# Seven products of quarter sums in place of eight in three groups of a down projection, computed in two column halves

## The chip, the cores and the metric

One Trainium2 chip, one core. The metric is the device time of one execution in microseconds (us). Engines are named as in the profile: PE (TensorE matmul), PEld (its weight loads), DVE (VectorE), ACT (ScalarE), POOL (GpSimd), SP (SyncE, which here only issues DMAs).

## What is computed

The reference is one layer of a hybrid decoder trunk on 256 tokens of 2048 features, in float32: a mixer part (gated linear attention and pooling, one combined input projection, one output projection), then a gated MLP, then a last RMS norm. The change lies in the MLP and the norm behind it:

```python
h = rmsnorm(x, norm_ffn_w[l])
gate, up = jnp.split(jnp.einsum('bsd,df->bsf', h, w_up[l]), 2, axis=-1)
gate = causal_dwconv(gate, conv_ffn_w[l]) + conv_ffn_b[l]
x = x + jnp.einsum('bsf,fd->bsd', jax.nn.gelu(gate, approximate=False) * up, w_down[l])
return rmsnorm(x, norm_final_w)
```

`w_up` is 2048 x 11264 and `w_down` is 5632 x 2048. The down projection multiplies the hidden values (256 x 5632) by `w_down`.

## The kernel before

Every float32 matrix product is made of three products in a rounded 32-bit format: each operand is split into a high and a low part, and high x high, low x high and high x low are summed in PSUM.

**Weights.** `srcs` lists all weight tiles of the kernel in the order in which they are used. One tile is 256 rows by 512 columns, held as 128 x 2 x 512. `load` (L125) brings it with one 512 KB DMA on SP's queue into `raw` (four buffers). `begin` makes two tiles of it: ACT copies it into `whi` (L158), and DVE subtracts to get `wlo` (L166). There are three buffers of each. `weights()` hands out the next pair and starts those two ahead (`AHEAD = 2`). So a tile's cast waits until PE has used the tile three before it.

**Order.** A scheduler fixes the order of instructions on each engine when the kernel is built, by its own estimate of times. On the chip each engine follows that order, and waits at semaphores.

**Up projection.** For each of 11 chunks of 512 features (four feature blocks of 128) `gemm_b` (L221, L222) forms the gate and then the up part, feature-major, 16 input blocks each, from the normalised features `fhl` (high and low part side by side, 16 blocks in one tile). DVE and ACT then do the convolution, the Gelu and the product (L1116 to L1128), and split the result `gs` into `hhi[c]` and `hlo[c]` (L1135, L1136), each 128 features x 4 blocks x 256 tokens.

**Down projection.** Here the hidden values are the stationary operand (128 features x 128 tokens) and the weights move, 512 columns at a time. The output is 4 columns of 512 by 2 token blocks of 128, and each of the 8 has a PSUM bank (`acc`: four from `psg`, four from `psm`). The loop runs over 22 pairs of feature blocks `kp` outside and over the four columns `c` inside, with one weight tile for each. `down_part` (L1154) uses a tile for both token blocks:

```python
for kk in range(2):
    k = 2 * kp + kk
    for n, (w, part) in enumerate(((hi, lh), (hi, ll), (lo, lh))):
        mm(ps[:, cs], part(k, t), w[:, kk, cs], ...)
```

That is 2 blocks x 3 passes x 2 token blocks = 12 products for a tile. The four tiles of the last pair are converted early (`KEEP`, `khi` and `klo`) and kept in buffers whose hidden values are no longer needed.

**End.** The last two pairs are done for one token block after the other, so that one block of tokens is normalised and stored while the other is multiplied. As a column's bank is complete, DVE adds it, scaled, to the residual `xt` (L1207), ACT squares and sums it (L1214), and DVE multiplies by the norm's weight `nfin` (L1216). The last block of 512 columns is done as two halves of 256. Then the sum of squares becomes the factor (L1203, L1204, L1211 on DVE, a power on POOL, L1217), the columns are scaled (L1182 to L1186) and stored (L1188).

Of the kernel before, what the change touches and what calls it, by code (L numbers as in the profile page):

```python
# [14 lines left out]
P = 128  # L15
# [20 lines left out]
def kernel(  # L36
# [32 lines left out]
    def nm(s):  # L69
        cnt[0] += 1  # L70
        return f"{s}_{cnt[0]}"
# [27 lines left out]
    LAST = KF // 2 - 1  # L99
    KEEP = (9, 12, 15, 18)  # L100
    kept = {}
    for kp in range(LAST):
        srcs += [down[c][kp] for c in range(4)]
        if kp in KEEP:
            kept[len(srcs)] = KEEP.index(kp)
            srcs.append(down[KEEP.index(kp)][LAST])
# [15 lines left out]
    def load_part(n, k):  # L122
        if n == len(loads):
            loads.append(wpool.tile(list(srcs[n].shape), F32, tag="raw", name=nm("raw"), bufs=4))
        last_load[0] = nc.sync.dma_start(loads[n][:, k], srcs[n][:, k]).ins  # L125

# [23 lines left out]
    def begin(n):  # L150
        while len(made) < min(len(srcs), n):
            load(len(made) + 1)
            raw = loads[len(made)]
            shape = list(raw.shape)
            keep = kept.get(len(made))
            hi = wpool.tile(shape, F32R, tag="whi", name=nm("whi")) if keep is None else \
                mtile(keep, shape, F32R, nm("khi"))
            nc.scalar.copy(hi, raw)  # L158
            if shape[1] == 8:
                lo = None  # L160
                nc.vector.tensor_tensor(hi[:, :, 32:64], raw[:, :, 0:32], hi[:, :, 0:32].bitcast(F32),
                                        op=ALU.subtract)
            else:
                lo = wpool.tile(shape, F32R, tag="wlo", name=nm("wlo")) if keep is None else \
                    mtile(4 + keep, shape, F32R, nm("klo"))
                last_split[0] = nc.vector.tensor_tensor(lo, raw, hi.bitcast(F32), op=ALU.subtract).ins  # L166
                splits.append(last_split[0])
            made.append((hi, lo))
# [123 lines left out]
    xhl = big.tile([P, KD, 2, S], F32R, tag="xhl", name="xhl")  # L292
    xhi, xlo = xhl[:, :, 0, :], xhl[:, :, 1, :]
# [11 lines left out]
    def parts_x(pts):  # L305
        for k, pt in pts:
            hi = nc.scalar.activation(xhi[:, k, :], pt, AF.Copy, scale=nmw[:, k : k + 1])
            lo = nc.vector.scalar_tensor_tensor(xlo[:, k, :], pt, nmw[:, k : k + 1], xhi[:, k, :].bitcast(F32),
                                                op0=ALU.mult, op1=ALU.subtract)
        return hi.ins, lo.ins  # L310
# [8 lines left out]
    def xh(k, t):  # L319
        return xhi[:, k, t * P : (t + 1) * P]  # L320

    def xl(k, t):
        return xlo[:, k, t * P : (t + 1) * P]
# [159 lines left out]
    for c in range(2):  # L483
        hi, lo = weights()
        for kk in range(8):
            k = 8 * c + kk
            mm(pba, hi[:, kk, :], xhl[:, k], start=(k == 0), stop=(k == KD - 1))
# [591 lines left out]
    fhl = big.tile([P, KD, 2, S], F32R, tag="xhl", name="fhl")  # L1079
    fhi, flo = fhl[:, :, 0, :], fhl[:, :, 1, :]  # L1080
    ssq4 = cpool.tile([P, 2, 4], F32, tag="ssq4", name="ssq4b")
    for c in range(4):
# [9 lines left out]
        for k2 in range(2):  # L1092
# [5 lines left out]
            for kk in range(2):  # L1098
                k = 4 * c + 2 * k2 + kk
                nw = vec[:, V_FFN + k : V_FFN + k + 1]  # L1100
                nc.scalar.activation(fhi[:, k, :], pt[:, kk, :], AF.Copy, scale=nw)
                nc.vector.scalar_tensor_tensor(flo[:, k, :], pt[:, kk, :], nw, fhi[:, k, :].bitcast(F32),
# [8 lines left out]
    hlo = []  # L1111
    rb2b = rb2.unsqueeze(1).to_broadcast([P, 4, S])
    for c in range(DFF // 512):
        ps = gemm_b(lambda k: fhl[:, k], KD)
# [12 lines left out]
        ps = gemm_b(lambda k: fhl[:, k], KD)  # L1127
# [10 lines left out]
        hlo.append(hl)  # L1138

    nfin = big.tile([P, D], F32, tag="xhl", name="nfin")  # L1140
    nc.scalar.dma_start(nfin, norm_final_w.partition_broadcast(P))
    acc = [[pg() for t in range(2)] for c in range(2)]
    for c in range(2):
        ps = pm()
        acc.append([ps[:, t, :] for t in range(2)])
    lh, ll = at(hhi), at(hlo)

    def down_part(kp, c, t, hi, lo, cs=slice(0, 512), ps=None, first=0):
        last_block = c == 3 and t == 1 and ps is None
        ps = acc[c][t] if ps is None else ps  # L1150
        for kk in range(2):
            k = 2 * kp + kk
            for n, (w, part) in enumerate(((hi, lh), (hi, ll), (lo, lh))):
                mm(ps[:, cs], part(k, t), w[:, kk, cs], start=(k == first and n == 0),  # L1154
                   stop=(k == KF - 1 and n == 2), skip_group_check=last_block)

    wk = []
    for kp in range(LAST - 1):
        for c in range(4):
            w = weights()  # L1160
            for t in range(2):
                down_part(kp, c, t, *w)
        if kp in KEEP:
            wk.append(weights())
    ws = []
    for c in range(4):
        ws.append(weights())
        if c == 0:
            for t in range(2):
                down_part(LAST - 1, c, t, *ws[c])  # L1170


    ssq5 = cpool.tile([P, 2, 5], F32, name="ssq5")
    part = cpool.tile([P, 2], F32, name="part")
    rs = cpool.tile([P, 2], F32, name="rsf")
    for t in range(2):
        ts = slice(t, t + 1)

        def scaled(c, by, queue):
            xs = xt[:, t, c * 512 : (c + 1) * 512]  # L1180
# [9 lines left out]


        blocks = [(c, slice(0, 512), None) for c in range(4 - t)]
        if t:
            blocks += [(3, slice(0, 256), None), (3, slice(256, 512), acc[0][0])]
        for n, (c, cs, ps) in enumerate(blocks):
            more = {} if ps is None else dict(ps=ps, first=2 * (LAST - 1))
            if c:
                down_part(LAST - 1, c, t, *ws[c], cs, **more)
            down_part(LAST, c, t, *wk[c], cs, **more)
            last = n == len(blocks) - 1  # L1200
            if last:

                nc.vector.tensor_reduce(part[:, ts], ssq5[:, t, 0:n], axis=mybir.AxisListType.X, op=ALU.add)  # L1203
                nc.vector.tensor_scalar(part[:, ts], part[:, ts], 1.0 / D, EPS, op0=ALU.mult, op1=ALU.add)  # L1204
            xs = xt[:, t, c * 512 : (c + 1) * 512]
            sums = cs if ps is not None else slice(0, 512)
            nc.vector.scalar_tensor_tensor(xs[:, sums], (acc[c][t] if ps is None else ps)[:, sums], rs2[:, ts],  # L1207
                                           xs[:, sums], op0=ALU.mult, op1=ALU.add)
            jk = cpool.tile([P, 512], F32, tag="sqj", name=nm("sqj"))
            if last:  # L1210
                nc.vector.tensor_tensor_reduce(jk[:, cs], xs[:, cs], xs[:, cs], scale=1.0 / D, scalar=part[:, ts],  # L1211
                                               op0=ALU.mult, op1=ALU.add, accum_out=rs[:, ts])
            else:
                nc.scalar.activation(jk[:, cs], xs[:, cs], AF.Square, accum_out=ssq5[:, t, n : n + 1])  # L1214
            if c < 3:
                nc.vector.tensor_tensor(xs, xs, nfin[:, c * 512 : (c + 1) * 512], op=ALU.mult)  # L1216
# [36 lines left out]
```

## Time and profile before

| what | value |
|---|---|
| device time, median of 3 runs | 1559.78 us (1559.38 to 1561.17) |
| span of the profiled execution | 1557.7 us |
| its own device time | not recorded apart; the median of the runs is 2.1 us above its span |
| PE busy | 1548.7 us (99%) |
| DVE busy | 1087.0 us (70%) |
| ACT busy | 748.2 us (48%) |
| HBM read and written | 299.66 MB and 5.28 MB |

The span runs from the first to the last instruction. In the rows of the profile, `out<-in` names tiles as the program does, `128x512` is partitions by elements, `x864` is the number of instructions, and what follows `<-` at the end is what ended the idle time before them. A line is that of the statement, and can be a helper's: L1154 is every product of the down projection.

### The profile page before, as it was taken

The page shows a single profiled execution, that of the slowest core. Times are in us where ns is not written, and L with a number is a line of the kernel's source. Part 1 is how long each engine was busy: PE and PEld are TensorE (multiplying, and loading weights), DVE is VectorE, ACT ScalarE, POOL GpSimd, SP SyncE. Part 2 cuts the span into 40 slices and gives each one's busy share as a digit, 9 for nine tenths or more (in the row PEclk, how much of TensorE's full clock was granted, in tenths as well). Part 3 has the DMA queues.
Part 4 walks back from the last instruction along what each step waited for, and adds up shares of the span by engine and source line. Part 5 has one row for each costly group of instructions (what it writes and reads, how often), then busy time and mean ns, then how long its engine had stood idle before and what let it go on. Part 6 is the DMA issues. An engine that isn't in the chain of part 4 may idle for free.

```text
span 1557.7 us, 21155 instructions
## 1 busy us (share of the span) xinstructions
PE 1548.7 (99%) x7966; PEld 1300.2 (83%) x7966; DVE 1087.0 (70%) x1676; ACT 748.2 (48%) x964; POOL 44.6 (3%) x54
## 2 busy tenths in 40 slices
PE   9999999999999999999999999999999999999998
PEld 8878888888878888888888888888888888888886
DVE  6788858996689859896656666776676667444445
ACT  6445446454545446354544544444444444434443
POOL 1010002000100000000000000000000000000000
PEclk9999999999999999999999999999999999999999
DMA  8776757766677656665655655555556656556662
GB/s 278 212 223 206 198 164 224 220 198 178 180 229 210 199 163 215 218 194 176 213 186 178 193 188 189 188 189 189 189 189 189 190 190 212 194 195 208 200 224 91
DMA packets 169108, 306.33 MB, mean 197 GB/s; under 512 B 19330, under 2 KB 23202, under 8 KB 168878
## 3 DMA queue, kind: packets, MB, share of 16 engines
q1 hardware_dynamic: 165984, 299.95, 61.4%
q10 hardware_dynamic: 3022, 5.03, 1.0%
q8 instruction: 62, 1.02, 0.3%
q14 instruction: 40, 0.33, 0.1%
HBM read 299.66 MB, written 5.28 MB: 196 GB/s over the span
## 4 chain that ended last, share of the span: by engine, by line
PE 98%; issue 1%; DMA 1%; DVE 0%; ACT 0%; POOL 0%; POOLq 0%; DVEq 0%
PE psm L199 15%; PE psm L197 15%; PE psm L198 15%; PE psm L221 11%; PE psg L221 10%; PE psg L1154 7%; PE psm L1154 7%; PE psg L222 5%; PE psm L222 5%; PE psm L333 1%; PE psg L242 1%; PE psg L723 1%; PE psg L725 0%; DMA vrow<-ev 0%; PE psg L861 0%
## 5 line engine op out<-in xcount | busy, mean ns | idle before, releaser
L166 DVE TENSOR_TENSOR wlo<-raw,whi 128x1024 fp32r<-128x1024 f32 x522 | 636.7, 1223 | 376.7 <-ACT whi L158 374.4
L158 ACT CAST whi<-raw 128x1024 fp32r<-128x1024 f32 x524 | 551.0, 1053 | 688.0 <-PE psm L198 282.7
L199 PE MATMUL psm<-wlo,xhl 128*128 128x512 f32 x864 | 339.6, 393 | 0.3 <-DVE wlo L166 0.3
L197 PE MATMUL psm<-whi,xhl 128*128 128x512 f32 x864 | 338.6, 392 | 0.0
L198 PE MATMUL psm<-whi,xhl 128*128 128x512 f32 x864 | 337.9, 391 | 0.0
L221 PE MATMUL psm<-fhl,whi 128*128 128x512 f32 x704 | 246.2, 396 | 0.0
L221 PE MATMUL psg<-fhl,whi 128*128 128x512 f32 x704 | 238.0, 394 | 0.0
L222 PE MATMUL psm<-fhl,wlo 128*128 128x256 f32 x704 | 194.3, 279 | 0.0
L199 PEld LDWEIGHTS psm<-wlo,xhl 128*128 128x128 f32 x864 | 162.3, 188 | 34.6 <-DVE wlo L166 1.5
L198 PEld LDWEIGHTS psm<-whi,xhl 128*128 128x128 f32 x864 | 162.3, 188 | 33.5
L197 PEld LDWEIGHTS psm<-whi,xhl 128*128 128x128 f32 x864 | 162.3, 188 | 33.3 <-issue 0.2
L222 PE MATMUL psg<-fhl,wlo 128*128 128x256 f32 x704 | 178.8, 279 | 0.0
L221 PEld LDWEIGHTS psm<-fhl,whi 128*128 128x128 f32 x704 | 131.4, 188 | 30.5
L221 PEld LDWEIGHTS psg<-fhl,whi 128*128 128x128 f32 x704 | 129.2, 188 | 24.1
L222 PEld LDWEIGHTS psg<-fhl,wlo 128*128 128x128 f32 x704 | 132.5, 188 | 6.9
L222 PEld LDWEIGHTS psm<-fhl,wlo 128*128 128x128 f32 x704 | 132.6, 188 | 1.1
L1154 PE MATMUL psg<-whi,hhi 128*128 128x512 f32 (+1 forms) x170 | 66.0, 388 | 0.0
L1154 PE MATMUL psg<-whi,hlo 128*128 128x512 f32 (+1 forms) x170 | 65.9, 388 | 0.0
L1154 PE MATMUL psm<-whi,hlo 128*128 128x512 f32 x168 | 65.1, 388 | 0.0
L1154 PE MATMUL psm<-wlo,hhi 128*128 128x512 f32 x168 | 65.1, 388 | 0.0
L1154 PE MATMUL psm<-whi,hhi 128*128 128x512 f32 x168 | 65.1, 388 | 0.0
L1154 PE MATMUL psg<-wlo,hhi 128*128 128x512 f32 (+1 forms) x170 | 59.6, 388 | 0.0
(278 smaller groups left out, 1505.9 us busy)
## 6 DMA issues: line engine op xcount, KB each, us to landing
raw<-in_w_in_dram SPq DMA_DIRECT2D x224, 512.0 KB, 4.2
raw<-in_w_up_dram SPq DMA_DIRECT2D x176, 512.0 KB, 4.5
raw<-in_w_down_dram SPq DMA_DIRECT2D x88, 512.0 KB, 4.3
raw<-in_w_out_dram SPq DMA_DIRECT2D x32, 512.0 KB, 3.6
mv<-vrow SPq DMA_DIRECT2D x12, 512.0 KB, 4.9
taps<-in_conv_qkv_w_dram SPq DMA_DIRECT2D x16, 256.0 KB, 6.4
raw<-in_pool_w_dram SPq DMA_DIRECT2D x8, 512.0 KB, 4.0
crow<-crd SPq DMA_DIRECT2D x4, 512.0 KB, 4.1
```

Of the source, the lines that this page charges most:

```text
L158: nc.scalar.copy(hi, raw)
L166: last_split[0] = nc.vector.tensor_tensor(lo, raw, hi.bitcast(F32), op=ALU.subtract).ins
L197: mm(ps[:, t, :], lh(k, t), hi[:, kk, :], start=(k == 0), stop=False)
L198: mm(ps[:, t, :], ll(k, t), hi[:, kk, :], start=False, stop=False)
L199: mm(ps[:, t, :], lh(k, t), lo[:, kk, :], start=False, stop=(k == nk - 1))
L221: mm(ps[f], hi[:, kk, fs], rhl(k), start=(k == 0), stop=False, skip_group_check=True)
L222: mm(ps[f][:, 1, :], lo[:, kk, fs], rhl(k)[:, 0, :], start=False, stop=(k == nk - 1), skip_group_check=True)
L242: nc.tensor.transpose(pt[:, ff, t * P : (t + 1) * P], src[:, t, f * P : (f + 1) * P], ident)
L333: mm(ps_k0[:, t, :], part(k, t), w[:, kk, :], start=(k == 0 and w is hi and part is xh), stop=(k == KD - 1 and w is lo))
L723: mm(pg0, kq[:, h, 0, 0:P], kq[:, h, :, :], start=True, stop=True)
L1154: mm(ps[:, cs], part(k, t), w[:, kk, cs], start=(k == first and n == 0), stop=(k == KF - 1 and n == 2), skip_group_check=last_block)
```

## The change

The up projection and everything before it stay as they are, except that the normalised features are held in four tiles (tags `x0` to `x3`) instead of one. Their buffers are used again later: `x0` for `nfin`, `x1` and `x2` for weights of the down projection, `x3` for sums of group 9.

The down projection is done in two halves of 1024 columns (two columns of 512 each): first half in all its feature blocks, then the second. Three of the 11 groups of four feature blocks, `SEVEN = (4, 9, 10)`, are computed in another way. For one group and one half, the hidden values are a 2 x 2 matrix of quarters (2 token blocks by 2 pairs of feature blocks) and the weights are another (2 pairs by 2 columns). Instead of eight products of quarters there are seven, of quarters or of sums of quarters (the Winograd form of Strassen's scheme):

- `half_sums` makes four sums of quarters of the hidden values on DVE and splits them into high and low parts. For group 4 this is done in the loop of the up projection, for 9 and 10 in the down projection.
- `quarter` loads the group's weights for a half with two DMAs of 1 MB, and DVE forms the differences `T1`, `T3`, `T2`, `T4` in place (the subtraction in `begin`), before the usual cast and split. Each of the seven tiles is used by one product of quarters only, 2 blocks x 3 passes = 6 matmul instructions.
- Four of the seven products are summed over the three groups in banks of their own (`11`, `T1`, `T2`, `T3`), the other three in the banks of the outputs they belong to. After the third group, DVE and ACT combine the four banks and add the results to `xt`.

The other eight groups are multiplied as before (`DIRECT`). Their weight tiles are put between the seven: one after each product but the first (`stream`, `PRODUCTS`, with `gaps` more ahead of each group: 4, 2, 2 in the first half and 3, 1, 1 in the second). In the second half the last two direct groups (8 tiles) are the end that is done for one token block after the other; four of its tiles are kept as before. The last 512 columns of the second token block are now cut into halves of 256 for all four of their tiles, before for two.

The core of the diff:

```diff
+    SEVEN = (4, 9, 10)
+    PRODUCTS = ("11", "21", "22", "T1", "T3", "T2", "T4")
+    DIRECT = [c for c in range(KF // 4) if c not in SEVEN]
...
+        for n, chunk in zip(gaps, SEVEN):
+            plain(n)
+            for i, what in enumerate(PRODUCTS):
+                steps[half].append(("part", chunk, what))
+                srcs.append((half, chunk, what))
+                if i:
+                    plain(1)
+        plain(len(todo))
+
+    ends = [(2 * d + j, c) for d in LAST for c in (2, 3) for j in range(2)]
+    stream(0, DIRECT, (4, 2, 2))
+    stream(1, DIRECT[:-2], (3, 1, 1), (9, 13, 17, 21))
+    srcs += [down[c][kp] for kp, c in ends[:4]]
...
+    def quarter(half, chunk, what):
+        if what == "11":
+            for j in range(2):
+                r = big.tile([P, 2, 1024], F32, tag=f"x{1 + j}", name=nm("quad"))
+                rows = slice((2 * chunk + j) * 256, (2 * chunk + j + 1) * 256)
+                last_load[0] = nc.sync.dma_start(r, w_down[0, rows, half * 1024 : (half + 1) * 1024]
+                                                 .rearrange("(k p) f -> p k f", p=P)).ins
+                for i in range(2):
+                    quarters[j, i] = r[:, :, 512 * i : 512 * (i + 1)]
+        b11, b12, b21, b22 = (quarters[j, i] for j in range(2) for i in range(2))
+        sums = {"T1": (b11, b12, b11), "T3": (b12, b22, b12), "T2": (b22, b22, b11), "T4": (b21, b21, b22)}
...
+            if isinstance(raw, tuple):
+                raw, plus, minus = raw
+                nc.vector.tensor_tensor(raw, plus, minus, op=ALU.subtract)
...
+    def half_sums(c):
+        h = whole[c]
+        a11, a12, a21, a22 = (h[:, 2 * j : 2 * j + 2, t * P : (t + 1) * P] for t in range(2) for j in range(2))
+        s = fp.tile([P, 4, S], F32, tag="y", name=nm("sums"))
+        s1, s2, s3, s4 = (s[:, n].rearrange("p (k s) -> p k s", k=2) for n in range(4))
+        nc.vector.tensor_tensor(s1, a21, a22, op=ALU.add)
+        nc.vector.tensor_tensor(s2, s1, a11, op=ALU.subtract)
+        nc.vector.tensor_tensor(s3, a11, a21, op=ALU.subtract)
+        nc.vector.tensor_tensor(s4, a12, s2, op=ALU.subtract)
...
+        nc.scalar.copy(hi, s)
+        nc.vector.tensor_tensor(lo, s, hi.bitcast(F32), op=ALU.subtract)
...
+    OPERAND = {"11": (0, 0), "21": (1, 0), "22": 3, "T1": 0, "T3": 2, "T2": 1, "T4": (1, 1)}
...
+            if chunk == SEVEN[-1] and what == PRODUCTS[-1]:
+                c0, c1 = 2 * hf, 2 * hf + 1
+                u = fp.tile([P, 2, 512], F32, tag="y", name=nm("u"))
+                u2, u3 = u[:, 0], u[:, 1]
+                nc.scalar.copy(u2, bank_of["11"])
+                plus(0, c0, bank_of["11"])
+                nc.vector.tensor_tensor(u2, u2, bank_of["T2"], op=ALU.add)
+                nc.vector.tensor_tensor(u3, u2, bank_of["T3"], op=ALU.add)
+                plus(1, c0, u3)
+                nc.vector.tensor_tensor(u2, u2, bank_of["T1"], op=ALU.add)
+                plus(0, c1, u2)
+                nc.vector.tensor_tensor(u3, u3, bank_of["T1"], op=ALU.add)
+                plus(1, c1, u3)
+        if hf == 0:
+            for c in range(2):
+                for t in range(2):
+                    plus(t, c, own[c, t])
+                    squared(t, c, c)
+                    weighted(t, c)
```

`plus` adds a bank or a sum, scaled, to the residual; `squared` and `weighted` are the old L1214 and L1216.

More of the change, by code (lines that the diff above doesn't have):

```diff
@@ L1176 @@
+    ws = []
+    for i in range(4):
+        ws.append(weights())
+        if i == 0:
+            for t in range(2):
+                direct(own[0, t], ends[0][0], t, ws[0], False, False)
+    ws += wk
+    late = pm()[:, 0]
     for t in range(2):
```

207 lines of the change are left out of this document (136 added, 71 removed).

## The prediction

> **What bounds the kernel now.** I read the page first (shares, slices, chain), then the groups of the last 258 us by shape, and then the timeline of the down projection engine by engine.
>
> ```profile
> span 1557.7 us, 21155 instructions
> ...
> PE 1548.7 (99%) x7966; PEld 1300.2 (83%) x7966; DVE 1087.0 (70%) x1676; ACT 748.2 (48%) x964; POOL 44.6 (3%) x54
> ...
> GB/s 278 212 223 206 198 164 224 220 198 178 180 229 210 199 163 215 218 194 176 213 186 178 193 188 189 188 189 189 189 189 189 190 190 212 194 195 208 200 224 91
> ...
> PE 98%; issue 1%; DMA 1%; DVE 0%; ACT 0%; POOL 0%; POOLq 0%; DVEq 0%
> ```
>
> The chain that ended last is TensorE nearly alone. The windows view, cut into the body of the down projection and its end, says the same of the stage that is changed (after the stretch: length, then busy time of PE, PEld, DVE, ACT, POOL, clock, DMA share, GB/s):
>
> ```profile
> 1312.00:1540.00 228.00, 228.00 (x1007) 188.81 (x1006) 110.93 (x96) 92.16 (x92) 0.00 (x0) 1.00 0.58 195
> 1540.00:1558.00 18.00, 10.08 (x56) 8.64 (x54) 9.97 (x22) 5.24 (x12) 1.10 (x2) 0.92 0.32 117
> ```
>
> PE is busy for 228 of 228 us at full clock; VectorE (DVE) is busy for 49% of it and ScalarE (ACT) for 40%. A busy PE alone proves little, since matmul records overlap. The Trainium skill says so too (Perfetto Trace Analysis, Identifying the Most-Contended Engine: matmul occupancy is not a good measure, weight-load occupancy is). By weight loads the stage stands at 83%, which would leave room without removing a product; what decides here is the distance between starts, in the timeline of PE:
>
> ```profile
> 1310.63 0.40 PE L1154 MATMUL psg<-whi,hlo 128*128 128x512 f32 x1
> ...
> 1314.49 0.39 PE L1154 MATMUL psm<-whi,hhi 128*128 128x512 f32 x1
> ...
> 1319.93 0.39 PE L1154 MATMUL psm<-whi,hhi 128*128 128x512 f32 x1
> ```
>
> Between the first and the third row stand 40 others, so 41 steps take 9.30 us: 0.2268 us for each product of 512 columns, without a gap. A product removed here is worth 0.2268 us, so long as its operands are never late. A weight tile that serves both token blocks (12 products) lasts 2.72 us on PE, a tile that serves one product of quarters (6 instructions) 1.36 us.
>
> **What the change removes.** Before, the stage has 44 feature blocks x 4 columns x 2 token blocks x 3 passes = 1056 products of 512 columns. In the change a group of four feature blocks and one column half takes 7 x 6 = 42 instead of 8 x 6 = 48. Three groups in two halves: 36 fewer, 36 x 0.2268 = **-8.17 us**. Before, the last block of columns is cut into halves of 256 for its last two weight tiles; after, for its last four:
>
> ```profile
> 1547.05 0.28 PE L1154 MATMUL psm<-whi,hhi 128*128 128x256 f32 x1
> ...
> 1549.81 0.28 PE L1154 MATMUL psg<-klo,hhi 128*128 128x256 f32 x1
> ```
>
> Those are 24 half products in 23 steps, 2.76 us, so 0.120 each; two of them cost 0.24 against 0.2268 for a whole one. Twelve more are cut: 12 x 0.0132 = **+0.16 us**. Behind the last product the same instructions follow (add, square and sum, power, scale, store), so the tail stays as it is: 0, with at most half a microsecond either way.
>
> Up to the down projection, the built order of the changed kernel is the same as before on PE, POOL and SP, instruction for instruction; splitting the normalised features into four tiles moves nothing. The load of the last norm's weights leaves ACT's queue some tiles earlier, at a place where ACT's next cast waits longer for PE than the load does: nothing. The one addition is the quarter sums of group 4 in the up projection: four DVE operations on 256 elements, one cast, one split.
>
> ```profile
> 1120.00:1180.00 60.00, 60.00 (x345) 52.34 (x345) 41.17 (x55) 29.89 (x37) 0.00 (x0) 1.00 0.59 186
> L166 DVE TENSOR_TENSOR wlo<-raw,whi 128x1024 fp32r<-128x1024 f32 x86 | 105.0, 1224 | 108.0 <-ACT whi L158 107.9
> L158 ACT CAST whi<-raw 128x1024 fp32r<-128x1024 f32 x86 | 90.4, 1054 | 125.1 <-PE psm L1154 60.1 <-PE psg L1154 58.8 <-PE psg L221 5.4
> L231 DVE TENSOR_TENSOR gs<-psg,lh 128x256 f32<-128x256 f32 x4 | 1.5, 416 | 0.0
> ```
>
> They cost 4 x 0.416 + 1.224 = 2.9 us of DVE once, where DVE is free for 19 of 60 us: nothing. The same rows price all that the change adds to DVE and ACT.
>
> **What it adds: conversions.** A weight tile is cast by ACT into its high part (1.05 us), then DVE subtracts to get the low part (1.22). In a group every product has its own tile, and four of the seven need a subtraction of quarters first. A group with its six ordinary tiles in between takes PE 7 x 1.36 + 6 x 2.72 = 25.9 us; DVE has 17 operations of 1.224 = 20.8 us (80%), ACT 13 x 1.054 = 13.7 us. So no engine is over-full, but DVE has 5 us to spare in 26 where it had half. Three tiles of each part exist: the cast of a tile starts when PE has left the tile three earlier. PE then works two tiles, 5.44 us before and 4.08 in a group, against 1.05 + 1.22 and some 0.2 for the hand-overs. 1.6 us are left, which one other DVE operation fits into and two do not. Two operations stand in the way at three places, by the order in which DVE has them.
>
> *First group, first half.* DVE carries the end of the up projection, the quarter sums of groups 9 and 10 and their splits as well. I follow it from the start of the stage: in the timeline above 18 products precede the one at 1314.49, so the stage starts at 1310.4.
>
> ```profile
> 1313.04 1.23 DVE L1128 TENSOR_TENSOR gs<-gs,y 128x1024 f32<-128x1024 f32 x1
> 1314.19 1.23 DVE L166 TENSOR_TENSOR wlo<-raw,whi 128x1024 fp32r<-128x1024 f32 x1
> 1315.39 1.23 DVE L1136 TENSOR_TENSOR hlo<-gs,hhi 128x1024 fp32r<-128x1024 f32 x1
> ```
>
> The first of these is done 3.8 us into the stage, and such operations start up to 1.20 apart when nothing holds them. In DVE's order the split of the group's first ordinary tile has seven large and four small operations ahead of it from there; it ends at 3.8 + 8 x 1.2 + 4 x 0.4 = 15.0. PE reaches the tile at 4 x 2.72 + 2 x 1.36 = 13.6 and needs the low part four products later, at 14.5: 0.5 us late. Further on the second quarter difference waits once more, by 0.4. After that PE is behind DVE. Taken: +1.0 us; from 0 (if hand-overs overlap) to 3.
>
> *Between the halves.* The four banks of the first half's own columns are added to the residual, squared and weighted, while the second half starts:
>
> ```profile
> L1216 DVE TENSOR_TENSOR xt<-xt,nfin 128x512 f32<-128x512 f32 x6 | 4.1, 689 | 2.7 <-ACT sqj L1214 2.7
> L1207 DVE SCALAR_TENSOR_TENSOR xt<-psm,rs,xt 128x512 f32<-128x512 f32 x4 | 3.0, 752 | 1.6 <-PE psm L1154 1.6
> ```
>
> 4 x 0.752 + 4 x 0.689 = 5.8 us of DVE over three ordinary tiles (8.2 us, with 3.7 us of their own splits), and the low part of the first group's first ordinary tile stands behind all of it: +0.3 us, from 0 to 2. The seven-product banks themselves are drained by eight such operations, 6 us under six ordinary tiles (16.3 us): nothing; uncovered, it would be those 6 us. In this drain DVE waits for PE's last sums with the next tile's split behind it, but the split is wanted only a tile and a half later.
>
> *Second and third group, second half.* The quarters are loaded as two 1 MB transfers into the buffers of the old ones. The second of them may start when the last quarter's low part is made, and in the second half only one ordinary tile separates the groups. On SP it also stands behind an ordinary load that waits for a later split; the ordinary loads behind it have four buffers and are wanted later. A 1 MB load on this queue is not in the trace; the nearest rows are these.
>
> ```profile
> raw<-in_w_down_dram SPq DMA_DIRECT2D x88, 512.0 KB, 4.3
> ...
> xt<-in_x_dram ACTq DMA_DIRECT2D x4, 512.0 KB, 7.9
> ```
>
> The bounds are 4.3 (as for half the size) and 8.6 us (twice it, near the 7.9 of four loads issued together); I take 4.3 + 0.52 MB at the 278 GB/s of the first slice (1.9) = 6.2. Counted from the start of the separating tile, the load is issued at -4.35 (PE leaves the tile three before at -6.8, cast and split follow), lands at 1.85, and behind it stand in order one cast (1.05), the split of the quarter, a quarter difference, the split of a kept tile and that of the ordinary tile (4 x 1.22). End: 7.8, with PE asking at 6.8. +1.0 us in the second group; in the third no kept tile and no other split stands between: 0. From 0 (at 4.3) to 3.4 + 2 (at 8.6). In the first half two ordinary tiles separate groups, 2.7 us more room: 0. By the Trainium skill (DMA: Bandwidth & Descriptors, Anatomy of one DMA: about 2.0 us plus bytes at 436 GB/s, fitted on another issue path) 1 MB would land in 4.4 us, an estimate; the sum would be 1.0 us lower, 1553.1. No row here shows that size, and for 512 KB the page gives 3.2 where the trace has 4.3.
>
> **Sum.** -8.17 + 0.16 + 1.0 + 0.3 + 1.0 = -5.7 us. Against the profiled execution: span 1557.7 - 5.7 = 1552.0. The median of the runs, 1559.78, is 2.1 us above that span; the same 2.1 on top gives 1554.1, rounded **1554.0 us**.
>
> **Rivals.** *The products go and nothing waits*: the three waits cancel because PE's order already takes the next tile's high parts while a low part is missing. Then -8.0: 1551.8. It is the near end of the forecast. I put the forecast, waits from 0 to 5 us in sum, at 0.75.
>
> *VectorE becomes the bound inside the groups.* For: 80% filled, long runs of splits in order, each behind a cast. Against: 5 us spare per group. If each of the 24 quarter-difference tiles brings PE a wait of 0.3 us, that is 7.2 more than no wait at all: 1551.8 + 7.2 = 1559.0, no change. 0.14, over 1556 to 1562; a third of it still faster.
>
> *The reloads of the quarters come too late* (the other side). Four groups reload right behind their predecessor: two with 6.2 us of room (second half) and two with about 9. At a landing time L each waits L - 6.2, or L - 9. The gain is gone where 2(L - 6.2) + 2(L - 9) = 8, at L = 9.6; at 11.6 us the sum is 16 and the kernel takes 1567.8. For it: the four loads issued together took 7.9, and each group asks for 2 MB within a few microseconds. Against it: the DMA share of the stage is 0.58, and a group moves 7 products' quarters and six tiles, 5.2 MB in 25.9 us, 202 GB/s against 195 now. PE would also stand still for over 2 us each time; in the last stretch above, with PE idle for 8 of 18 us, the clock falls to 0.92. The Trainium skill (TensorE: Matmul & The Clock Gate, Why this matters for your kernels) warns of gaps over about 3 us, after which the clock starts at half; with waits as forecast no gap comes near it. 0.11.
>
> **How the numbers follow.** About 0.2% (3.1 us) is what a measurement of this kernel can tell from no change. Faster by more: the forecast's 0.75 and 0.04 of the VectorE rival, 0.79. Within: 0.10. Slower: 0.11, all of it the reloads. The range starts a little under the sum without waits, 1551.5, and runs to 1558.5, which takes in the larger bounds of two of the three waits (3 + 2 + 1.5 over 1551.8) and half of the VectorE rival; the reloads' case and the rest lie outside.
>
> **What would show it.** In the profile after: no time between products except at three places. The windows view over the down stage shows PE full, DVE near 150 us busy instead of 111 (24 differences, 16 sums of banks and two sets of quarter sums more, six splits fewer), ACT little more, the DMA share as before, clock 1.00. PE's waits name the splits of low parts, 1 us at the first group and 1 us near the second group of the second half, and no bank. A PE that waits for ACT casts of quarters, which wait for a DMA, would be the reload rival; many small waits on splits the VectorE one. A distance between starts other than 0.227 us in the products of quarters, a clock under 1.00, or a shorter or longer stage before the down projection would make the prediction wrong in its base.

## The result, and the profile after

| what | before | after |
|---|---|---|
| device time, median | 1559.89 us (1559.38 to 1561.17, 5 runs) | 1552.77 us (1551.17 to 1555.42, 5 runs) |
| span of the profiled execution | 1557.7 us | 1550.4 us |
| device time of that execution | not recorded apart | 1552.15 us |
| products of the down projection, first start to last start | 239.51 us | 231.66 us |

The ratio after to before is 0.9956, with a 95% interval of 0.9944 to 0.9969: 7.1 us faster. The forecast was 1554.0 us, 1551.5 to 1558.5.

First the page of after: span, shares, slices of VectorE, the shares of the chain that ended last, and the issues of the two kinds of weight loads (instructions, KB each, median us from issue to landing).

```profile
span 1550.4 us, 21200 instructions
...
PE 1541.6 (99%) x7942; PEld 1294.1 (83%) x7942; DVE 1151.4 (74%) x1749; ACT 770.3 (50%) x987; POOL 39.3 (3%) x54
...
DVE  6788858996689858886656667767666677877885
...
PE 98%; issue 1%; DMA 1%; DVE 0%; ACT 0%; POOL 0%; POOLq 0%; ACTq 0%
...
raw<-in_w_down_dram SPq DMA_DIRECT2D x64, 512.0 KB, 4.6
...
quad<-in_w_down_dram SPq DMA_DIRECT2D x12, 1024.0 KB, 6.2
```

TensorE still bounds alone, though VectorE has 64 us more to do (1151.4 against 1087.0). The stage that was changed, in the windows view (length, then busy time of PE, PEld, DVE, ACT, POOL, clock, DMA share, GB/s):

```profile
1312.00:1533.00 221.00, 221.00 (x976) 182.49 (x975) 175.95 (x169) 115.58 (x120) 0.00 (x0) 1.00 0.57 190
1533.00:1551.00 18.00, 10.20 (x68) 9.26 (x66) 7.29 (x15) 3.91 (x8) 1.10 (x2) 0.84 0.32 117
```

PE is again busy for all of the body at full clock, while VectorE fills 80% of it. The ends of the stage, in the timeline of PE (start, duration, instruction), after and then before:

```profile
1311.14 0.28 PE L273 MATMUL psg<-fhl,wlo 128*128 128x256 f32 x1
1311.26 0.40 PE L1247 MATMUL psm<-whi,hhi 128*128 128x512 f32 x1
...
1542.92 0.28 PE L1247 MATMUL psm<-klo,hhi 128*128 128x256 f32 x1
```

```profile
1310.16 0.28 PE L222 MATMUL psg<-fhl,wlo 128*128 128x256 f32 x1
1310.30 0.50 PE L1154 MATMUL psg<-whi,hhi 128*128 128x512 f32 x1
```

With the row of before at 1549.81, the stage went from 1549.81 - 1310.30 = 239.51 to 1542.92 - 1311.26 = 231.66 us, 7.85 less. What lies behind the last product went from 1557.7 - 1549.81 = 7.9 to 1550.4 - 1542.92 = 7.5, 0.4 less. The up projection ended 0.96 us later. Together that is -7.3, the difference of the spans. The 0.96 need not be the change's. The instructions of PE before that point stand in the same order in both kernels but for one product near 1055 us, which stands some places later in after. By 490 us, far ahead of it, PE is 0.7 us later already. And in the six runs below whose order on PE up to there is that of after, the stage starts anywhere from 1310.01 to 1312.67.

From the first start to the last lie 996 whole products of 0.2268 us and 47 half ones of 0.120, 231.53 us. So 0.13 us of the stage are not products, and the timeline has nearly all of them in one place, between 1466.4 and 1468.1. What caused them is told where the prediction is answered.

### The profile page after: what moved, and what is told of

It reads as the page before. It is cut to its first block, busy times and chain, and to the rows that moved or that the text cites. A ratio compares the mean times of both kernels' runs of the same rounds, so it can differ in the third digit from the quotient of the medians.

```text
span 1550.4 us, 21200 instructions
## 1 busy us (share of the span) xinstructions
PE 1541.6 (99%) x7942; PEld 1294.1 (83%) x7942; DVE 1151.4 (74%) x1749; ACT 770.3 (50%) x987; POOL 39.3 (3%) x54
## 4 chain that ended last, share of the span: by engine, by line
PE 98%; issue 1%; DMA 1%; DVE 0%; ACT 0%; POOL 0%; POOLq 0%; ACTq 0%
PE psm L250 15%; PE psm L248 15%; PE psm L249 15%; PE psm L272 11%; PE psg L272 11%; PE psm L1247 7%; PE psg L1247 7%; PE psg L273 5%; PE psm L273 5%; PE psm L391 1%; PE psg L293 1%; PE psg L781 1%; PE psg L783 0%; DMA vrow<-ev 0%; PE psm L309 0%
## 5 line engine op out<-in xcount | busy, mean ns | idle before, releaser
L209 ACT CAST whi<-raw 128x1024 fp32r<-128x1024 f32 x500 | 526.0, 1052 | 612.9 <-PE psm L249 281.8
L217 DVE TENSOR_TENSOR wlo<-raw,whi 128x1024 fp32r<-128x1024 f32 x498 | 607.3, 1222 | 287.6 <-ACT whi L209 284.5
L209 ACT CAST whi<-quad 128x1024 fp32r<-128x1024 f32 x42 | 44.3, 1054 | 47.5 <-PE psm L1247 27.6
L217 DVE TENSOR_TENSOR wlo<-quad,whi 128x1024 fp32r<-128x1024 f32 x42 | 51.3, 1222 | 18.0 <-ACT whi L209 17.3
L1247 PE MATMUL psm<-whi,hhi 128*128 128x512 f32 (+1 forms) x150 | 58.0, 387 | 0.0
L1247 PE MATMUL psm<-whi,hlo 128*128 128x512 f32 (+1 forms) x150 | 58.0, 386 | 0.0
L1247 PE MATMUL psm<-wlo,hhi 128*128 128x512 f32 (+1 forms) x150 | 57.8, 386 | 0.0
L248 PE MATMUL psm<-whi,mhi 128*128 128x512 f32 x128 | 50.9, 397 | 0.0
```

The source lines that it names most:

```text
L248: mm(ps[:, t, :], lh(k, t), hi[:, kk, :], start=(k == 0), stop=False)
L1247: mm(ps[:, cs], lhs(kk), part_[:, kk, cs], start=(first and kk == 0 and n == 0), stop=(last and kk == 1 and n == 2), skip_group_check=shared)
```

## The experiments

In all of them the down projection is judged by two numbers: the time, and the stage from its first to its last product, 231.66 us in after. "Lag" is the time from the first product less the products so far at 0.2268 and 0.120 us. Where a run has a ratio it is to the kernel before, on the same chip.

**The two halves alone, no group of seven** (`e_halves`).

```diff
-    SEVEN = (4, 9, 10)
+    SEVEN = ()
...
-        if c == SEVEN[0]:
+        if SEVEN and c == SEVEN[0]:
```

> Column halves in the new order, but no group by seven products: all 11 groups take eight. Theory (the gain is the removed products and nothing else): 1056 products as before, so the time of before plus 0.16 us for the twelve more products cut into two of 256 columns: 1560.0 us, ratio to before 1.000; first to last product of the down projection 239.7 us. Rival (part of the gain comes from the new order of columns and banks, or from an earlier start of the output): 1555 to 1558.

Measured: 1561.46 us, ratio 1.0007 (0.9998 to 1.0016); the stage takes 241.46 us. The column halves bring nothing; the gain is in the groups. The stage is even 1.8 us longer than its products, because of kept tiles (`khi`) whose loads come late. The timelines of ACT and PE of this run show the larger of two such waits (the bracket is idle time before the instruction, and what ended it):

```profile
1481.19 1.05 ACT L209 CAST khi<-raw 128x1024 fp32r<-128x1024 f32 x1 [5.11 <-DMA raw<-in_w_down_dram]
```

```profile
1483.24 0.50 PE L1247 MATMUL psg<-whi,hhi 128*128 128x512 f32 x1 [0.62 <-ACT whi L209]
```

ACT stood 5.1 us at a cast that PE did not need for long, and three casts that PE needed soon stood behind it.

**The same with the kept tiles further apart** (`e_halves_k`).

```diff
-    stream(1, DIRECT[:-2], (3, 1, 1), (9, 13, 17, 21))
+    stream(1, DIRECT[:-2], (3, 1, 1), (10, 15, 20, 25))
```

> The column halves without any group of seven products, as in the run before of the two halves alone, but with the four kept tiles of the end loaded after 10, 15, 20 and 25 ordinary tiles of the second half instead of 9, 13, 17 and 21. Theory (the 1.8 us by which that run's down projection was longer than its products came from the kept tile whose load waited for a buffer and held up ScalarE's queue): with the tiles further apart the stage takes 239.7 us and the kernel 1559.6, the time before. Rival (the wait belongs to the column halves themselves, in the change-over): the stage stays at 241.5 and the time at 1561.4.

Measured: 1559.70 us, ratio 0.9994 (0.9985 to 1.0003), stage 239.62 us: the 1.8 us are gone, as the first theory had it. So 239.6 to 231.66 is what the three groups bring, 7.96 us, where 36 products are 8.17 (the cut columns are the same in both).

**Two groups instead of three** (`e_two`).

```diff
-    SEVEN = (4, 9, 10)
+    SEVEN = (4, 9)
...
-    stream(0, DIRECT, (4, 2, 2))
-    stream(1, DIRECT[:-2], (3, 1, 1), (9, 13, 17, 21))
+    stream(0, DIRECT, (4, 2))
+    stream(1, DIRECT[:-2], (3, 1), (9, 13, 17, 21))
```

> Two groups (4 and 9) by seven products instead of three. Theory: 24 products fewer than before, 24 x 0.2268 = 5.4 us less, plus 0.16: 1554.6 us, ratio 0.9966. Rival (a fixed gain or cost of the new order, whatever the number of groups): the same as with three groups, 1552.8, or a smaller share of it.

Measured: 1556.05 us, ratio 0.9972 (0.9962 to 0.9982), stage 235.30 us: 4.3 below the halves alone. The 24 products would be 5.4; 1.1 is lost, nearly all of it in one wait at the second group of the second half. PE waits for the cast of an ordinary tile. Ahead of it on ACT stand a quarter that landed late and then a kept tile that landed late as well (timelines of PE and ACT):

```profile
1470.05 0.50 PE L1247 MATMUL psg<-whi,hhi 128*128 128x512 f32 x1 [0.73 <-ACT whi L209]
```

```profile
1465.43 1.05 ACT L209 CAST whi<-quad 128x1024 fp32r<-128x1024 f32 x1 [3.41 <-DMA quad<-in_w_down_dram]
1468.00 1.05 ACT L209 CAST khi<-raw 128x1024 fp32r<-128x1024 f32 x1 [1.51 <-DMA raw<-in_w_down_dram]
1468.95 1.04 ACT L209 CAST whi<-raw 128x1024 fp32r<-128x1024 f32 x1
```

That is the place at which the prediction had put its third wait. There, two groups lose 1.0 us where three lose 0.13.

**Groups without ordinary tiles between them** (`e_packed`): the reload of the quarters loses its cover. The one ordinary tile behind a group's last product is counted as the group's own, and stays.

```diff
-    stream(0, DIRECT, (4, 2, 2))
-    stream(1, DIRECT[:-2], (3, 1, 1), (9, 13, 17, 21))
+    stream(0, DIRECT, (4, 0, 0))
+    stream(1, DIRECT[:-2], (3, 0, 0), (9, 13, 17, 21))
```

> Three groups as in the change, but no ordinary tiles between the groups (gaps 4, 0, 0 and 3, 0, 0), so that the quarters of the next group are asked for 5.4 us earlier in the first half and 2.7 us earlier in the second, measured from the issue of their load. In the change the casts of the second quarters began 8.1 and 8.8 us after the issue in the first half, 6.1 and 5.8 in the second. Theory (a 1 MB load needs some 6.2 us and there is hardly any room): each cast is late by 2.7 to 3.6 us, less what the splits have in hand, together 8 to 11 us: 1561 to 1564 us. Rival (the loads are hidden anyway, since other loads move out of their way): 1553 us.

Measured: 1559.02 us, ratio 0.9992 (0.9982 to 1.0001), stage 238.51 us: 6.85 more than after, a little under the expected 8 to 11, and nearly all of the gain. The waits view names the transfer, and the timelines of ACT and PE show how it passes on:

```profile
ACT whi L209 <- DMA quad<-in_w_down_dram: 12.8, 4, 4.9
```

```profile
1465.74 1.04 ACT L209 CAST whi<-quad 128x1024 fp32r<-128x1024 f32 x1 [4.89 <-DMA quad<-in_w_down_dram]
```

```profile
1466.83 0.50 PE L1247 MATMUL psg<-whi,hhi 128*128 128x512 f32 x1 [1.41 <-ACT whi L209]
```

Four reloads, four places of waiting (about 0.4, 1.6, 3.0 and 2.0 us of lag). The order of the tiles is a part of the gain, not a detail.

**One load buffer fewer** (`e_raw3`).

```diff
-    loads.append(wpool.tile(list(srcs[n].shape), F32, tag="raw", name=nm("raw"), bufs=4))
+    loads.append(wpool.tile(list(srcs[n].shape), F32, tag="raw", name=nm("raw"), bufs=3))
```

> The changed kernel with three buffers for ordinary weight loads instead of four, so that each ordinary load waits for the split of one tile later; the second load of a group's quarters, which stands behind such a load on SyncE's queue, is then issued later too, as the prediction had assumed. (The order of some instructions before the down projection moves with it, so the down projection's own length decides: 231.66 us in the changed kernel.) Theory (the wait of 1 us forecast at the second group of the second half did not come because the load ahead was released early enough): there the issue moves from 1.2 us before the cast of the kept separating tile's neighbours to about 2.4 us later, behind the next ordinary tile's split, and PE waits 1 to 2.5 us near that group, with 0 to 2 us at the other reloads: a stage of 233 to 236 us. Rival (the chain behind the landing is what counts and the issue has over 2 us of slack): stage 231.7 to 232.2 us, and the time of the changed kernel, 1552.8.

Measured: 1559.82 us, ratio 0.9996 (0.9987 to 1.0006). In the profiled execution, whose span is 9.3 us longer than that of after, the down projection starts 8.0 us later (1319.27); that was not followed up. The stage takes 232.88 us. For the question asked, the run decides nothing: the second load of the second group's quarters went out at 1464.42, 9.30 us later than in after, and PE is 9.30 us later there too (8.01 from the start and 1.29 of lag). Relative to PE the issue had not moved, since the order of loads on SP moved with the buffers. But the lag itself is of use. It arises at one place, in the first group (PE, then DVE):

```profile
1335.00 0.50 PE L1247 MATMUL psm<-wlo,hhi 128*128 128x512 f32 x1 [1.00 <-DVE wlo L217]
```

```profile
1333.73 1.22 DVE L217 TENSOR_TENSOR wlo<-raw,whi 128x1024 fp32r<-128x1024 f32 x1
```

This is the split of the group's first ordinary tile, the place of the prediction's first wait. Here it starts 14.46 us into the stage, in after 13.19.

**The second load of the quarters later by one or two VectorE operations** (`e_late1`, `e_late2`; one execution each, so only stages are compared). N is 1 and 2.

```diff
+                for _ in range(N if srcs[len(made)] in ((1, 4, "T4"), (1, 9, "T4")) else 0):
+                    nc.vector.tensor_tensor(lo, raw, hi.bitcast(F32), op=ALU.subtract)
                 nc.vector.tensor_tensor(lo, raw, hi.bitcast(F32), op=ALU.subtract)
```

> The changed kernel with one split done twice in each of two places of the second half: that of the last quarter (T4) of the first and of the second group, behind which the second load of the next group's quarters waits. The load goes out 1.1 us later there, and VectorE, idle for 1.0 and 0.6 us just behind, takes the extra operation without delaying its next ones by much. Theory (the forecast's wait of 1 us at the second group did not come because the load went out 1.5 us earlier than taken; its chain of landing, cast, split and difference was right and was just met): PE waits about 1.1 us at the second group and 0 to 0.5 at the third: a stage of 232.7 to 233.3 us, against 231.66. Rival (the chain has room and the load's landing is hidden anyway): 231.7 to 232.0.

> As e_late1 with the same two splits done three times: the second loads go out 2.3 us later. Theory: each microsecond by which the load is later is a microsecond of PE at the second group: 2.2 us there and 0.5 to 1.5 at the third, a stage of 234.3 to 235.4 us. Rival (room in the chain): 231.7 to 232.5.

Measured: stages of 234.31 and 239.20 us, both above what either theory gave. At the second group the load goes out at 1456.66 and 1458.50 instead of 1455.12; with the shift of PE itself taken out, that is 1.3 and 3.5 us later. PE loses 0.4 and 2.2 us there. So there were some 0.9 to 1.3 us of room, and then a microsecond late was nearly a microsecond lost. But this is not the room of after, since the added operations had changed the built order. In after a kept tile's cast stands ahead of the one of the group's first ordinary tile, and its split too; in both runs they stand behind, which makes the way to the ordinary tile's split one operation shorter. ACT of after, then of the first of the two:

```profile
1464.29 1.05 ACT L209 CAST khi<-raw 128x1024 fp32r<-128x1024 f32 x1 [2.06 <-DMA raw<-in_w_down_dram]
1465.24 1.05 ACT L209 CAST whi<-raw 128x1024 fp32r<-128x1024 f32 x1
```

```profile
1464.16 1.05 ACT L209 CAST whi<-raw 128x1024 fp32r<-128x1024 f32 x1
1465.73 1.05 ACT L209 CAST khi<-raw 128x1024 fp32r<-128x1024 f32 x1 [0.52 <-DMA raw<-in_w_down_dram]
```

At the third group the loads (1488.63 and 1490.61 instead of 1483.84) were 4.3 and 4.9 us later relative to PE as it stood ahead of that group, not 1.1 and 2.3. The order had changed there as well: in after the last quarter is split ahead of a kept tile, and in these runs its last split stands behind one. DVE of after, then of the first of the two:

```profile
1482.59 1.23 DVE L217 TENSOR_TENSOR wlo<-quad,whi 128x1024 fp32r<-128x1024 f32 x1 [1.26 <-ACT whi L209]
1484.10 1.23 DVE L217 TENSOR_TENSOR klo<-raw,khi 128x1024 fp32r<-128x1024 f32 x1 [0.29 <-ACT khi L209]
```

```profile
1483.11 1.22 DVE L218 TENSOR_TENSOR wlo<-quad,whi 128x1024 fp32r<-128x1024 f32 x1 [1.27 <-ACT whi L209]
1486.25 1.23 DVE L219 TENSOR_TENSOR klo<-raw,khi 128x1024 fp32r<-128x1024 f32 x1 [1.92 <-ACT khi L209]
1487.39 1.22 DVE L219 TENSOR_TENSOR wlo<-quad,whi 128x1024 fp32r<-128x1024 f32 x1
```

PE's losses there were 2.3 and 5.5 us. In the first run 1.3 of the 2.3 came before that load had gone out, behind a kept tile's cast that stood waiting for its own load (ACT of that run):

```profile
1485.16 1.05 ACT L209 CAST khi<-raw 128x1024 fp32r<-128x1024 f32 x1 [2.09 <-DMA raw<-in_w_down_dram]
```

In the second run some 1.6 us of them came with a lower clock (PE of that run):

```profile
1498.95 0.50 PE L1249 MATMUL psg<-whi,hhi 128*128 128x512 f32 x1 [2.80 <-ACT whi L209]
...
1500.97 0.63 PE L1249 MATMUL psg<-wlo,hhi 128*128 128x512 f32 x1
1501.40 0.63 PE L1249 MATMUL psg<-whi,hhi 128*128 128x512 f32 x1
1501.83 0.63 PE L1249 MATMUL psg<-whi,hlo 128*128 128x512 f32 x1
```

**Splits done twice** for the 24 tiles that are differences (`e_split24`) or for all 42 tiles of quarters (`e_split42`): a price on VectorE alone.

```diff
 e_split24
+                for _ in range(srcs[len(made)][2][0] == 'T' if isinstance(srcs[len(made)], tuple) else 0):
 e_split42
+                for _ in range(isinstance(srcs[len(made)], tuple)):
 both
+                    nc.vector.tensor_tensor(lo, raw, hi.bitcast(F32), op=ALU.subtract)
                 nc.vector.tensor_tensor(lo, raw, hi.bitcast(F32), op=ALU.subtract)
```

> The changed kernel, with the split of a tile done twice for the 24 tiles that are differences of quarters (T1, T3, T2, T4) and once for the other 18 quarters: 21 VectorE operations for a group and half instead of 17. Theory (VectorE's slack in a group is its pitch of 1.14 us against PE's 25.9 us, 21 x 1.14 = 23.9): the operations fit and the time is that of the changed kernel, 1552 to 1554, but for the places where the tile waits in a chain of cast, difference, two splits (3.6 us and the cast against 4.08): up to 0.3 us each at 24 places, at most 1560. Rival (the forecast's: two operations in the way cost about 1 us, every time): each difference tile has two in the way, 24 x 0.5 to 1.0 us = 12 to 24 us, so 1565 to 1577. Rival (the loss is proportional to the work added, as with all 42 splits doubled, 28 of 48 us): 24 x 1.14 x 0.6 = 16 us, 1569.

> As in the change, but the split of each of the 42 quarter tiles is done twice on VectorE with the same result. A group then has 24 VectorE operations. At the distance of 1.14 us that they keep back to back that is 27.4 us against 25.9 of TensorE, so 1.5 us for each of six groups, part of it recovered by the ordinary tiles between: 1556 to 1562 us. Theory of the forecast (1.22 each and waits at single tiles): 29.3 us a group, 20 us in all: 1573. Rival (VectorE runs far enough ahead, only TensorE counts): 1553.

Measured: with 24, 1556.50 us, ratio 0.9974 (0.9963 to 0.9985), stage 236.12; with 42, 1581.21 us, ratio 1.0135 (1.0122 to 1.0149), stage 261.26. So 24 operations more cost 4.5 us of stage, and 42 cost 29.6. With 24 the time is within the first theory's bounds: a group has 21 operations, 21 x 1.134 = 23.8 us in PE's 25.9, and four of the six groups lose 0.3 us or less. The rest is in the two groups with tight places, 2.0 us in the first and 2.3 in the second group of the second half, where the order had changed as in the delayed runs. With 42 the time lies above all three expectations. A group has 24 operations, 27.2 us, which is 1.3 over, or 8 us in six groups. The other 22 were not shared out one by one. Two things in them can be seen: the quarters' reload goes out later (the second load of the second group in the second half at 1473.93, about 3.6 us later relative to PE than in after) and is waited for, and the clock falls (waits of the run with 42, then a window of it):

```profile
ACT whi L209 <- DMA quad<-in_w_down_dram: 16.0, 4, 5.4
```

```profile
1486.00:1492.00 6.00, 5.47 (x13) 3.80 (x12) 5.50 (x5) 1.05 (x1) 0.00 (x0) 0.50 0.51 172
```

**A fourth group** (`e_four`): group 8 as well, an ordinary tile only after the fourth to the seventh product. The hidden values of the first groups are kept without the quarter that no product needs, for space.

```diff
-    SEVEN = (4, 9, 10)
+    SEVEN = (4, 8, 9, 10)
...
-                if i:
+                if i in after:
...
-    stream(0, DIRECT, (4, 2, 2))
-    stream(1, DIRECT[:-2], (3, 1, 1), (9, 13, 17, 21))
+    stream(0, DIRECT, (3, 2, 2, 2), (3, 4, 5, 6))
+    stream(1, DIRECT[:-2], (2, 1, 1, 0), (3, 4, 5, 6), (9, 12, 15, 18))
```

> The changed kernel with a fourth group (8) by seven products: 12 products of 512 columns fewer, so only four ordinary tiles are left between the seven tiles of a group (after the fourth to the seventh product) and fewer ahead of each group (3, 2, 2, 2 and 2, 1, 1, 0). Theory (only products count as long as quarters and VectorE keep up): -12 x 0.2268 = -2.7 us, 1550.0 if nothing waits. Rival (the margins found for packed groups and doubled splits): a group lasts 7 x 1.36 + 4 x 2.72 = 20.4 us on PE and VectorE has 15 to 16 operations in it, 17 to 18.5 us, and the quarters of the last group are reloaded with no ordinary tile between: 1.4 to 2.8 us wait there and 1 to 3 us elsewhere, in sum 3 to 6 us, so 1553 to 1556, no gain over three groups.

Measured: 1557.67 us, ratio 0.9982 (0.9973 to 0.9991), stage 236.27 us. Twelve products fewer would make it 231.66 - 2.72 = 228.94, so 7.3 us of waits have come in, more than the 3 to 6 expected. 1.6 us of lag is there by 1441, and the rest comes from 1450 on, in the second half, where ACT waits up to 4.3 us for the quarters and PE behind it (waits view, then PE):

```profile
ACT whi L209 <- DMA quad<-in_w_down_dram: 7.5, 2, 4.3
```

```profile
1504.08 0.50 PE L1261 MATMUL psg<-whi,hhi 128*128 128x512 f32 x1 [0.79 <-ACT whi L209]
```

Removing products paid up to three groups; a fourth, with the fewer ordinary tiles that it leaves between the products of quarters, cost 4.6 us of stage. Neither this version nor any other run here beats the changed kernel.

## Why the prediction was right, and where its terms were off

**The sum's large term held.** 36 products at 0.2268 us and twelve more cut ones at +0.0132 gave -8.01. The stage lost 7.85 with 0.13 us of waits in it, so 7.98 without them. That no product of quarters takes longer than an ordinary one, and that weight loads at 83% left no other bound, follows from a stage equal to its products. The tail, put at 0 within half a microsecond, gave 0.4.

**The three waits were oversized: 2.3 us taken, 0.1 measured.** This is the error of the forecast, and it leaves the result between the forecast and its rival without waits (1551.8). That the time came within 1.2 us of the forecast is partly luck: stage and tail together lost 8.2 us where 5.7 were forecast, and the 0.96 us by which the stage started later took some of that back. The prediction had put this term at nothing, with an order on PE that was the same instruction for instruction, and had named a longer stretch before the down projection as a sign against its base. The first and the third wait had the right place and a wrong margin, the second did not come at all:

*First group, 1.0 us taken.* The step that failed is the pitch of VectorE, taken as 1.20 us from two neighbouring rows. DVE and PE of after:

```profile
1324.45 1.22 DVE L217 TENSOR_TENSOR wlo<-raw,whi 128x1024 fp32r<-128x1024 f32 x1
...
1326.26 1.22 DVE L217 TENSOR_TENSOR wlo<-quad,whi 128x1024 fp32r<-128x1024 f32 x1
1327.39 1.22 DVE L217 TENSOR_TENSOR wlo<-raw,whi 128x1024 fp32r<-128x1024 f32 x1
```

```profile
1325.83 0.40 PE L1247 MATMUL psm<-wlo,hhi 128*128 128x512 f32 x1
```

Operations with nothing to wait for start 1.13 us apart and overlap by 0.09. Over eight of them that is 0.5 us, all of the lateness that was forecast; the four small ones, 0.34 apart where 0.4 was taken, give 0.2 more. The split ends at 1325.67 and PE uses it at 1325.83. The run with three load buffers shows the same split 1.27 us later and a PE that waits 1.0 us for it, so the place was rightly chosen.

*Between the halves, 0.3 us taken.* Nothing was lost there: the lag moves by less than 0.05 us from 1400 to 1450. The first of the eight operations ran from 1424.45, while PE began the second half only at 1426.97, and the split that was to stand behind all eight ended at 1437.87, 0.9 us before PE used it (1438.76).

*Second group of the second half, 1.0 us taken.* The landing time was right (6.2 us taken, 6.2 the median, 5.95 for this load). What failed is the time of issue: "on SP it also stands behind an ordinary load that waits for a later split". SP's and DVE's timelines of after:

```profile
1455.12 0.37 SPq L167 DMA_DIRECT2D quad<-in_w_down_dram  x1
```

```profile
1453.87 1.23 DVE L217 TENSOR_TENSOR wlo<-quad,whi 128x1024 fp32r<-128x1024 f32 x1 [0.47 <-ACT whi L209]
```

The load went out as the last quarter's split ended, about 1.5 us earlier than taken, since the ordinary load ahead of it had been released by an earlier split. The chain behind the landing was as forecast. In after the quarter's split starts at 1462.26, and three more operations at 1.134 us and the length of the last would end at 1466.9, some 0.8 us ahead of the time at which PE asks (about 1467.8, with 0.1 for the hand-over). A load 1.5 us later would so have cost about 0.7 us, an estimate from these rows, so that the larger part of the forecast's 1.0 was an error of where in SP's queue the waiting stood. The delayed runs do not price it, since their order was another.

The 0.13 us that after does lose near 1467 has another cause, which the prediction had not: not the quarters, but the kept tile. ACT stood 2.06 us at its load with the ordinary tile's cast behind it (the two rows of ACT above), DVE waited with the kept tile's split, and the ordinary tile's split ended at 1467.74, just as PE asked for it. DVE and PE of after:

```profile
1465.38 1.23 DVE L217 TENSOR_TENSOR klo<-raw,khi 128x1024 fp32r<-128x1024 f32 x1 [0.76 <-ACT khi L209]
1466.52 1.22 DVE L217 TENSOR_TENSOR wlo<-raw,whi 128x1024 fp32r<-128x1024 f32 x1
```

```profile
1467.87 0.42 PE L1247 MATMUL psg<-wlo,hhi 128*128 128x512 f32 x1
```

**VectorE's load was miscounted.** The prediction said near 150 us busy and six splits fewer; the window has 176. A group and half has seven tiles to split instead of four, 18 more in six of them, so 24 operations of 1.22 us (29 us) were left out. The groups view of after shows them in the stage:

```profile
L217 DVE TENSOR_TENSOR wlo<-raw,whi 128x1024 fp32r<-128x1024 f32 x59 | 72.1, 1222 | 19.5 <-ACT whi L209 18.4
L217 DVE TENSOR_TENSOR wlo<-quad,whi 128x1024 fp32r<-128x1024 f32 x42 | 51.3, 1222 | 18.0 <-ACT whi L209 17.3
L204 DVE TENSOR_TENSOR quad<-quad 128x1024 f32<-128x1024 f32 x12 | 14.7, 1222 | 0.2
L204 DVE TENSOR_TENSOR quad<-quad,quad 128x1024 f32<-128x1024 f32 x12 | 14.6, 1219 | 0.0
```

It did not change the sum, because the working by groups had counted 17 operations in 25.9 us rightly.

**The rivals.** VectorE as the bound did not come, and the doubled splits show by how much: four more operations to a group cost 0.3 us or less in four groups and about 2 us in each of two (4.5 in all), seven cost five microseconds on the mean (29.6 in six). The reloads' rival did not come either, but its mechanism is real and near. Taking the ordinary tiles away from between the groups brings it in (6.85 us), and in the delayed runs a load late by more than about a microsecond does. By the prediction's own formula two reloads had 6.2 us of room and two about 9; the median landing took those 6.2. Its remark on the clock holds as well: a stop that cost 2.96 us (3.19 between two starts, less a product) cost some 1.6 us more by a reduced clock. The Trainium skill's rule (TensorE: Matmul & The Clock Gate, Why this matters for your kernels), gaps over about 3 us and then a start at half, agrees with that row in the half and nearly in the length (PE was idle for 2.80 us), but not in the moment: the first products after it kept their usual pace.

## What to carry to other kernels

Where one engine runs without a gap, price an arithmetic saving by the distance between starts, and then ask which operand comes late; here the saving paid until one did. For such margins use the distance between starts of neighbouring operations that wait for nothing, not their duration, and follow each load to the instruction that releases it, including the loads ahead of it in its queue. A busy share says little about slack: here VectorE at 80% took four more operations per group at almost no cost in four groups of six and failed at seven, and a change of the order of tiles or one extra group gave most of the gain back (6.85 and 4.6 of 7.85 us).

## What was not expected of the hardware

The clock's fall comes late and after short stops too. In the run with the loads later by two operations PE started no product between 1495.76 and 1498.95, ran at its usual pace until 1500.7, and only then took 0.43 us for a product instead of 0.227, until about 1504.3. With 42 doubled splits no stop around 1480 cost more than 1.9 us, yet the window from 1486 to 1492 stands at a clock of 0.50; just ahead of it, three stops of 1.9, 0.4 and 1.3 us lay within five microseconds. Several short waits close together can thus bring what a longer one does. They need not: in the run without ordinary tiles stops of 1.6, 0.7 and 0.3 us from 1465 to 1470.4 were followed by a window at 1.00 (1470 to 1476). Where the limit lies was not measured.

A cast for later use can hold up a cast for now: ACT stood 5.1 us at a kept tile's load with three urgent casts behind it, and moving four places in the list of tiles took away 1.8 us. It is the same that cost after its 0.13 us near 1467.
